# A streaming-encoder layer on one core: u projected first by neighbouring tokens and turned through DRAM, v second

## The chip, the core and the metric

The kernel runs on one core of a Trainium2 chip. The metric is the device time of one execution in microseconds (us), the median of several runs; less is better. A core has a matrix engine (TensorE, PE in the profile; its weight loads are listed apart as PEld), a vector engine (VectorE, DVE), an activation engine (ScalarE, ACT), a general engine (GpSimd, POOL) and a queue engine (SyncE, SP) that only issues transfers. Each engine works its instructions off in the order in which the program lists them. ScalarE and GpSimd can issue transfers too; such an instruction then stands in that engine's own order.

## What is computed

One residual layer of 1024 tokens with 1024 channels: two parallel token mixers on one normalised input, then cross-attention into 256 memory tokens, then a gated MLP. What matters here is the first projection and what is done with two of its parts.

```python
h = rms_norm(x, norm_mix_pre)                  # x * rate(token) * gain(channel)
q, k, v, u, gate_logits = split(h @ w_in)      # v and u: 512 columns each
o_attn = stick_breaking_attention(q, k, v)
ug = u.reshape(1, S, 32, 16)                   # 32 groups of 16 channels
bu = einsum('gpc,bsgc->bsgp', b_bar, ug)       # then a scan over the 1024 tokens
o_ssm = ...                                    # read out, + d * u, gelu, GLU
```

The rate of a token (one over the root of its mean square) is a factor of a whole row of h, so the kernel multiplies with it after the product, not before.

## The kernel before, in words

Every float32 product is made of three matmuls of rounded halves: `mm3` (L141) multiplies high by high (L142), high by low (L143) and low by high (L144). The first stage holds the transposed input `hT` (channels on the partitions, tokens along the row) and makes two passes over it. In a pass, `tokens(now, n, i, k)` (L427) is called for 8 token tiles i and 8 channel tiles k. 128 columns of `hT` are the stationary operand, 512 columns of weights the moving one, and the sum lies in one of six PSUM banks `ps_m`. So one pass has 8 x 8 x 3 = 192 matmuls of 128x512.

- Pass n = 0 makes v. Tile i takes tokens i*128 to i*128+127, which lie side by side in `hT`. `put` (L438) has ScalarE scale the sum by the rates of the tile (`rates_x`, one per partition) into a row buffer `vr` (L443), and SP writes it to DRAM (`v_d`, L444). Attention loads it from there much later (`values`, L985).
- Pass n = 1 makes u. The state-space branch wants eight neighbouring tokens in one partition. So tile i takes the tokens i, i+8, i+16, ... (`slice(i, S, 8)`, L429), whose columns of `hT` lie 8 elements (32 bytes) apart, and `put` writes straight into the tile `U` (L440). Its rates are needed in the same order: they go from `rates_x` to DRAM (`rx_d`, L409) and come back as `r8` (L410).

`rates_out` (L406) also issues the load of `row_k` (L411, issued at L280), a row of rates that attention needs later. `mem_rates_out` (L505) writes the rates of the memory tokens to DRAM. All these are issued by SP.

The four weight chunks of each pass come through four buffers (tag `wr`, `w_load` L378). ScalarE rounds them to the high half (L389) and VectorE makes the low half (L393). The two tiles of the memory tokens (`mem_load`, L495) use the same four buffers afterwards.

While the second pass runs on PE, VectorE and ScalarE prepare the state-space tables (`tables` L644, `operators` L663, `readout` L675). After it PE runs gate projections (`gate_job` L284, weights cast at L256, low half at L260), and between them in fixed slots the state-space steps: `flip_u` (L715) transposes groups of `U`, `states` (L730) multiplies and starts a scan on VectorE (L744 to L756), `outputs` (L762) reads it out.

The order of the work on PE, ScalarE, VectorE and GpSimd is written out by hand: `at(t, go)` (L228) puts a piece of work on a list with a planned time, and `all_events` (L232) emits the list in the order of these times. The planned times fix the order only; an engine starts its next instruction as soon as what it waits for is there. The order on SP is chosen by the compiler's own scheduler.

The times that the change uses are planned times too. The second pass begins at `u_begin` (52.4), the chunks' low halves are planned from L819 on, and the pass ends about 47 later.

Of the kernel before, what the change touches and what calls it, by code (L numbers as in the profile page):

```python
# [11 lines left out]
F32 = mybir.dt.float32  # L12
F32R = mybir.dt.float32r
BF16 = mybir.dt.bfloat16
AF = mybir.ActivationFunctionType
# [5 lines left out]
P = 128  # L21
S = 1024
# [23 lines left out]
def kernel(ctx: ExitStack, tc: tile.TileContext, a: dict, out: bass.AP, dbg=None):  # L46
    nc = tc.nc
    V, G, C, T = nc.vector, nc.gpsimd, nc.scalar, nc.tensor
    dma = nc.sync.dma_start
# [3 lines left out]
    dpool = ctx.enter_context(tc.tile_pool(name="dpool", bufs=1, space=DRAM))  # L53
    ha = ctx.enter_context(tc.tile_pool(name="ha", bufs=4, side="left"))

    v_d = dpool.tile([S, 512], F32, name="v_d")
    os_d = dpool.tile([4, P, S], F32, name="os_d")
    oa_d = dpool.tile([4, P, S], F32, name="oa_d")
    ol_d = dpool.tile([4, P, S], F32, name="ol_d")
# [9 lines left out]
    zcol = const.tile([P, 1], F32, name="zcol")  # L69
# [7 lines left out]
    wr = ExitStack()  # L77
    pr_ = wr.enter_context(tc.tile_pool(name="pr", bufs=1, side="left"))
    row_k = pr_.tile([P, 512], F32, name="row_k")
    gcol = pr_.tile([P, 2, KT], F32, name="gcol")  # L80
    rates_x = pr_.tile([P, 2, KT], F32, name="rates_x")
    rates_m = pr_.tile([P, 2], F32, name="rates_m")
    pr_.tile([P, 88], F32, name="pad_r")
    rx_d = dpool.tile([KT, P], F32, name="rx_d")
    rm_d = dpool.tile([2, P], F32, name="rm_d")
# [16 lines left out]
    def ps(tag):  # L102
        pool, w, n = psum[tag]
        return pool.tile([P, w], F32, tag=tag, name="ps_" + tag, bufs=n)
# [36 lines left out]
    def mm3(acc, sh, sl, mh, ml, first, last):  # L141
        T.matmul(acc, sh, mh, start=first, stop=False)  # L142
        T.matmul(acc, sh, ml, start=False, stop=False)  # L143
        T.matmul(acc, sl, mh, start=False, stop=last)  # L144
# [83 lines left out]
    def at(t, go):  # L228
        heapq.heappush(events, (t, len(seen), go))
        seen.append(t)  # L230
# [48 lines left out]
    def rates_load(h):  # L279
        dma(row_k, rx_d[4 * h:4 * h + 4].rearrange("t p -> (t p)").partition_broadcast(P))  # L280
# [57 lines left out]
    def h_hi(k, sl):  # L338
        return hT[0][k // 4][:, k % 4, sl]

    def h_lo(k, sl):
        return hT[1][k // 4][:, k % 4, sl]

    def g3(ap):
        return ap.rearrange("p (g c) -> p g c", c=16)

    wx = ExitStack()
    px = wx.enter_context(tc.tile_pool(name="px", bufs=1, side="left"))
# [3 lines left out]
    pa = ra.enter_context(tc.tile_pool(name="pa", bufs=1, side="right"))  # L352
    r0 = ExitStack()
    p0 = r0.enter_context(tc.tile_pool(name="p0", bufs=1, side="right", reuse_waits="tile"))
# [4 lines left out]
    U = pa.tile([P, 32, 8, 16], F32, name="U")  # L359
# [4 lines left out]
    xt, rows_x, raw, pair = {}, {}, {}, {}  # L364
# [12 lines left out]

    def w_load(n, c):  # L378
        raw[n, c] = px.tile([P, 1024], F32, tag="wr", name="wr", bufs=4)
        dma(raw[n, c], a["w_in_N"][n, c])  # L380

    def w_pair(n, c):
        if c == 3:
# [17 lines left out]
        V.tensor_scalar(r, sums_x[:, t:t + 1], 1.0 / D, EPS, op0=ALU.mult, op1=ALU.add)  # L401
        G.tensor_tensor(rates_x[:, 0, t:t + 1], r, mhalf, op=ALU.pow)

    r8 = pa.tile([P, 8], F32, name="r8")

    def rates_out():  # L406

        V.tensor_scalar(rates_x[:, 1], rates_x[:, 0], -1.0, None, op0=ALU.mult)
        dma(rx_d.rearrange("t p -> p t"), rates_x[:, 0])  # L409
        dma(r8, rx_d.rearrange("t (q r) -> (t q) r", r=8))  # L410
        rates_load(0)  # L411

    def gained(t, kk):
        ks = slice(0, KT) if kk is None else slice(4 * kk, 4 * kk + 4)
# [11 lines left out]

    def tokens(now, n, i, k):  # L427

        sl = slice(i * P, (i + 1) * P) if n == 0 else slice(i, S, 8)  # L429
        if k == 0:  # L430
            accs_[n, i] = ps("m")
        acc = accs_[n, i]
        wh, wl = (w[:, (k % 2) * 512:(k % 2 + 1) * 512] for w in pair[n, k // 2])
        mm3(acc, h_hi(k, sl), h_lo(k, sl), wh, wl, k == 0, k == KT - 1)
        if k < KT - 1:
            return

        def put(t):  # L438
            if n:
                C.activation(U[:, :, i, :], g3(acc), AF.Identity, bias=zcol, scale=r8[:, i:i + 1])  # L440
                return
            vt = p0.tile([P, 512], F32, tag="vr", name="vr", bufs=3)
            C.activation(vt, acc, AF.Identity, bias=zcol, scale=rates_x[:, 0, i:i + 1])  # L443
            dma(v_d[i * P:(i + 1) * P, :], vt)  # L444

        at(now + STEP + (0.2 if n else 7.0), put)

# [28 lines left out]
    def begin_of(t):  # L476
        return FIRST + 16 * STEP + 8 * STEP * (t - 2)

    u_begin = begin_of(KT)

    for t in range(KT):
        s0 = begin_of(t)
        if t > 1:
            for kk, go, dt_ in ((None, gained, 3.6), (0, x_high, 2.35), (1, x_high, 1.75), (0, x_low, 1.7), (1, x_low, 1.0)):
                at(s0 - dt_, lambda _, go=go, t=t, kk=kk: go(t, kk))
        if t + 4 < KT:
            at(s0 + (2.0 if t > 1 else 12.0), lambda _, t=t: x_load(t + 4))
# [15 lines left out]
        G.tensor_tensor(rates_m[:, i:i + 1], r, mhalf, op=ALU.pow)  # L503

    def mem_rates_out():  # L505
        dma(rm_d.rearrange("t p -> p t"), rates_m)

    line(70.0, (lambda: mem_load(0), 0), (lambda: mem_load(1), 16.0), (lambda: mem_rate(0), 1.4), (lambda: mem_rate(1), 2.6),
         (mem_rates_out, 0))
# [16 lines left out]
    turns = pa.tile([P, 7, 32], F32, name="turns")  # L526
    pr = pa.tile([P, 32, 9], F32, name="pr")
    pi = pa.tile([P, 32, 9], F32, name="pi")
    pa.tile([P, 96], F32, name="pad_a")

    def constants():
        G.memset(ec, math.e)
# [282 lines left out]
    u_begin = clock  # L815
# [58 lines left out]
    while timed:  # L874
        t0, _, took, go, n = heapq.heappop(timed)
# [70 lines left out]
    for m in range(4):  # L946
        j = glu_job(m)
# [165 lines left out]
    t, nf, begun, last_z = 0.0, 0, {}, 1e9  # L1113
# [393 lines left out]
    for n, (ch, go, args, last) in enumerate(steady):  # L1507
        while timed and timed[0][0] <= clock + STEP / 2:
            _, _, took, turn_, x = heapq.heappop(timed)
# [17 lines left out]
    while timed:  # L1527
        _, _, took, turn_, x = heapq.heappop(timed)
# [633 lines left out]
    for s in range(last + 1):  # L2162
        prep()
        w, r = 1 + s // 7, s % 7
# [60 lines left out]
    for prod in (2, 1, 5, 6, 3, 7):  # L2225
        acc = bank_b if prod in (2, 5, 3) else bank_a
        for k in range(NF // 2):
# [11 lines left out]
            elif i2 == 4:  # L2239
# [3 lines left out]
                r8 = ExitStack()  # L2243
# [107 lines left out]
```

## Time and profile before

| | us |
|---|---|
| median of 3 runs | 1651.96 (1651.85 to 1652.86) |
| the profiled execution | 1653.66 |
| its span, first to last instruction | 1651.9 |
| PE busy in it | 1632.3 |
| VectorE busy in it | 1163.5 |
| ScalarE busy in it | 880.3 |
| mean granted TensorE clock | 0.996 of full speed |

The profile comes from one execution. It lists busy time by engine, groups of instructions by line, the waits between engines, and a timeline. In a timeline row stand the start, the length, the engine, the line, the operation, what is written and read, and in brackets how long the engine had been idle and what ended that. Times in the views count from the first instruction.

### The profile page before, as it was taken

Reading aid. Unit: us, or ns where it says so; the run is one execution under the profiler, and the core shown is the slowest. Engines: PE = TensorE matmul, PEld = TensorE weight load, DVE = VectorE, ACT = ScalarE, POOL = GpSimd, SP = SyncE. Lnnn points to the kernel's source line nnn. Section 1 sums busy time; section 2 is a strip of 40 time slices with the busy share of each in tenths; the row PEclk is TensorE's granted clock in tenths of the full one; section 3 lists DMA queues with packets and bytes.
Section 4 is the critical chain, followed back from the end, with each engine's and each line's share of the span. In section 5 each row is a group of like instructions: output and inputs, shape, how many; then the busy total and the mean of one; then the engine's idle time right before and its main releaser. Section 6 shows DMA issues by size and latency. Waiting matters only on the chain.

```text
span 1651.9 us, 22414 instructions
## 1 busy us (share of the span) xinstructions
PE 1632.3 (99%) x8062; PEld 1383.0 (84%) x8062; DVE 1163.5 (70%) x1616; ACT 880.3 (53%) x1459; POOL 202.2 (12%) x296
## 2 busy tenths in 40 slices
PE   9999999999999999999999999999999999999998
PEld 7998888888888988888888888878888888888886
DVE  7778637776867688467555678888887788775473
ACT  5434346676766544345444556556555556654441
POOL 5000002333332000011000000111111111000010
PEclk9999999999999999999999998999999999999999
DMA  9412144232433964464323684677777676688672
GB/s 328 120 46 66 59 145 111 71 102 78 115 99 125 334 198 134 166 217 153 140 65 128 225 274 153 194 207 214 210 198 201 186 203 187 208 301 290 192 236 82
DMA packets 125439, 279.26 MB, mean 169 GB/s; under 512 B 23696, under 2 KB 28304, under 8 KB 125200
## 3 DMA queue, kind: packets, MB, share of 16 engines
q1 hardware_dynamic: 113664, 251.35, 46.2%
q0 software_dynamic: 9360, 18.09, 6.2%
q10 hardware_dynamic: 2304, 8.39, 1.3%
q8 instruction: 63, 1.03, 0.3%
q14 instruction: 48, 0.39, 0.1%
HBM read 203.98 MB, written 67.38 MB: 164 GB/s over the span
## 4 chain that ended last, share of the span: by engine, by line
PE 90%; DVE 5%; DMA 2%; ACT 2%; issue 1%; SPq 0%; POOL 0%; DVEq 0%; ACTq 0%; POOLq 0%
PE ps_p L1928 8%; PE ps_p L1927 8%; PE ps_p L1926 8%; PE ps_f L142 7%; PE ps_f L144 6%; PE ps_f L143 6%; PE ps_d L2198 4%; PE ps_d L2196 4%; PE ps_d L2197 4%; PE ps_m L143 3%; PE ps_m L142 3%; PE ps_m L144 3%; PE ps_o L1070 2%; PE ps_w L1045 2%; PE ps_z L142 1%; PE ps_z L144 1%
## 5 line engine op out<-in xcount | busy, mean ns | idle before, releaser
L142 PE MATMUL ps_f<-hT,wh 128*128 128x512 f32 x384 | 161.2, 420 | 0.0
L144 PE MATMUL ps_f<-hT,wl 128*128 128x512 f32 x384 | 150.8, 393 | 0.0
L143 PE MATMUL ps_f<-hT,wh 128*128 128x512 f32 x384 | 150.6, 392 | 0.0
L1927 PE MATMUL ps_p<-qS,bm 128*128 128x512 f32 (+2 forms) x368 | 141.5, 384 | 1.7 <-DVE qS L1751 1.7
L1926 PE MATMUL ps_p<-qS,bm 128*128 128x512 f32 (+2 forms) x368 | 141.4, 384 | 1.0 <-DVE uu L1944 1.0
L1928 PE MATMUL ps_p<-qS,bm 128*128 128x512 f32 (+2 forms) x368 | 141.5, 384 | 0.0
L148 DVE TENSOR_TENSOR dn<-raw,dn 128x1024 fp32r<-128x1024 f32 x77 | 93.6, 1223 | 63.6 <-ACT dn L147 61.1
L147 ACT CAST dn<-raw 128x1024 fp32r<-128x1024 f32 x77 | 80.6, 1052 | 86.9 <-PE ps_d L2198 40.0
L2196 PE MATMUL ps_d<-dn 128*128 128x512 f32 x308 | 119.8, 389 | 0.0
L2197 PE MATMUL ps_d<-dn 128*128 128x512 f32 x308 | 119.8, 389 | 0.0
L2198 PE MATMUL ps_d<-dn 128*128 128x512 f32 x308 | 119.8, 389 | 0.0
L1031 POOL TENSOR_TENSOR s<-s,s 128x127 f32<-128x127 f32 (+4 forms) x96 | 89.8, 936 | 223.1 <-DVE s L1025 175.5
L1928 PE MATMUL ps_p<-qA,bm 128*128 128x512 f32 (+2 forms) x272 | 105.3, 387 | 0.5 <-DVE bm L1857 0.5
L1926 PE MATMUL ps_p<-qA,bm 128*128 128x512 f32 (+2 forms) x272 | 105.5, 388 | 0.0
L1927 PE MATMUL ps_p<-qA,bm 128*128 128x512 f32 (+2 forms) x272 | 105.3, 387 | 0.0
L1939 ACT COPY uu<-ps_p 128x512 f32<-128x512 f32 (+2 forms) x90 | 51.5, 572 | 92.3 <-PE ps_p L1928 92.3
L1869 POOL DMA_DIRECT2D bm<-in_ffn_up_T x61 | 52.7, 864 | 358.7 <-ACT bm L1868 149.6
L144 PEld LDWEIGHTS ps_f<-hT,wl 128*128 128x128 f32 x384 | 72.1, 188 | 16.1
L1019 ACT ACTIVATE s<-ps_z,rates_x 128x128 f32<-128x128 f32 (+3 forms) x96 | 56.3, 586 | 53.7 <-PE ps_z L1008 48.2
L1927 PEld LDWEIGHTS ps_p<-qS,bm 128*128 128x128 f32 x368 | 70.2, 191 | 15.0 <-DVE qS L1751 2.0
L1926 PEld LDWEIGHTS ps_p<-qS,bm 128*128 128x128 f32 x368 | 70.1, 191 | 14.5 <-ACT uu L1939 1.4
L1928 PEld LDWEIGHTS ps_p<-qS,bm 128*128 128x128 f32 x368 | 70.3, 191 | 13.3 <-DVE bm L1857 0.2
(544 smaller groups left out, 4459.5 us busy)
## 6 DMA issues: line engine op xcount, KB each, us to landing
raw<-sd SPq DMA_DIRECT2D x77, 256.0 KB, 4.0
bm<-in_ffn_up_T POOLq DMA_DIRECT2D x61, 256.0 KB, 5.4
ws<-in_w_in_T SPq DMA_DIRECT2D x24, 512.0 KB, 3.5
ws<-in_xa_wo_N SPq DMA_DIRECT2D x23, 512.0 KB, 4.1
wv<-in_ffn_up_T SPq DMA_DIRECT2D x22, 512.0 KB, 4.1
wg<-in_ffn_up_T SPq DMA_DIRECT2D x22, 512.0 KB, 3.9
dr<-in_ffn_down SPq DMA_DIRECT2D x22, 512.0 KB, 6.6
td<-st SPq DMA_DIRECT2D x44, 256.0 KB, 6.1
```

Of the source, the lines that this page charges most:

```text
L142: T.matmul(acc, sh, mh, start=first, stop=False)
L143: T.matmul(acc, sh, ml, start=False, stop=False)
L144: T.matmul(acc, sl, mh, start=False, stop=last)
L147: C.copy(dh, src)
L148: (lo or V).tensor_tensor(dl, src, f(dh), op=ALU.subtract)
L1031: G.tensor_tensor(s1[:, n0:e], s1[:, n0:e], s2[:, n0 + 1:e + 1], op=ALU.mult)
L1926: T.matmul(acc, bm[:, 0, ks], q[:, 0, k, cs], start=alone and k == 0, stop=False, skip_group_check=True)
L1927: T.matmul(acc, bm[:, 0, ks], q[:, 1, k, cs], start=False, stop=False, skip_group_check=True)
L1928: T.matmul(acc, bm[:, 1, ks], q[:, 0, k, cs], start=False, stop=k == 3, skip_group_check=True)
L2196: T.matmul(acc[i], v[:, 0, 0, sl], v[:, 0, 1], start=first, stop=False, skip_group_check=True)
L2197: T.matmul(acc[i], v[:, 0, 0, sl], v[:, 1, 1], start=False, stop=False, skip_group_check=True)
L2198: T.matmul(acc[i], v[:, 1, 0, sl], v[:, 0, 1], start=False, stop=last, skip_group_check=True)
```

## The change

Pass n = 0 now makes u and pass n = 1 makes v: the weights are taken in the other order, and both passes take neighbouring tokens. The rows of u are written to a new DRAM tensor `u_d` from the first pass. Four loads (`steps_load`, SP) bring them back with eight neighbouring tokens per partition, 128 columns each, through the `wr` buffers, and four copies on ScalarE (`steps_put`) put them into `U`. The rows of v go to `v_d` from the second pass through one buffer `vt`, which the gate projections use after it. `r8` and its load are gone. The write of the token rates, the load of `row_k` and the write of the memory rates are issued by ScalarE, the first two at later planned times. A padding tile grows by what `r8` took.

```diff
     v_d = dpool.tile([S, 512], F32, name="v_d")
+    u_d = dpool.tile([S, 512], F32, name="u_d")
...
     def w_load(n, c):
         raw[n, c] = px.tile([P, 1024], F32, tag="wr", name="wr", bufs=4)
-        dma(raw[n, c], a["w_in_N"][n, c])
+        dma(raw[n, c], a["w_in_N"][1 - n, c])
...
-    r8 = pa.tile([P, 8], F32, name="r8")
-
     def rates_out():
 
         V.tensor_scalar(rates_x[:, 1], rates_x[:, 0], -1.0, None, op0=ALU.mult)
-        dma(rx_d.rearrange("t p -> p t"), rates_x[:, 0])
-        dma(r8, rx_d.rearrange("t (q r) -> (t q) r", r=8))
-        rates_load(0)
+        at(60.0, lambda _: C.dma_start(rx_d.rearrange("t p -> p t"), rates_x[:, 0]))
+        at(78.0, lambda _: C.dma_start(row_k, rx_d[0:4].rearrange("t p -> (t p)").partition_broadcast(P)))
...
-        sl = slice(i * P, (i + 1) * P) if n == 0 else slice(i, S, 8)
+        sl = slice(i * P, (i + 1) * P)
...
         def put(t):
-            if n:
-                C.activation(U[:, :, i, :], g3(acc), AF.Identity, bias=zcol, scale=r8[:, i:i + 1])
-                return
-            vt = p0.tile([P, 512], F32, tag="vr", name="vr", bufs=3)
+            vt = (pa.tile([P, 512], F32, tag="vt", name="vr", bufs=1) if n else
+                  p0.tile([P, 512], F32, tag="vr", name="vr", bufs=3))
             C.activation(vt, acc, AF.Identity, bias=zcol, scale=rates_x[:, 0, i:i + 1])
-            dma(v_d[i * P:(i + 1) * P, :], vt)
+            dma((v_d if n else u_d)[i * P:(i + 1) * P, :], vt)
...
+    rows_u = {}
+
+    def steps_load(o):
+
+        rows_u[o] = px.tile([P, 8, 128], F32, tag="wr", name="ur", bufs=4)
+        dma(rows_u[o], u_d[:, 128 * o:128 * o + 128].rearrange("(j r) c -> j r c", r=8))
+
+    def steps_put(o):
+        C.copy(U[:, 8 * o:8 * o + 8].rearrange("p g r c -> p r g c"), rows_u[o].rearrange("p r (g c) -> p r g c", c=16))
+
+    for o in range(4):
+        at(u_begin + (14.0, 16.5, 27.5, 33.5)[o], lambda _, o=o: steps_load(o))
+        at(u_begin + (24.0, 30.0, 36.0, 42.0)[o], lambda _, o=o: steps_put(o))
...
     def mem_rates_out():
-        dma(rm_d.rearrange("t p -> p t"), rates_m)
+        C.dma_start(rm_d.rearrange("t p -> p t"), rates_m)
...
-    pa.tile([P, 96], F32, name="pad_a")
+    pa.tile([P, 104], F32, name="pad_a")
```

## The prediction

> **What bounds the kernel now.** I read the page first: the span and the busy times.
>
> ```profile
> span 1651.9 us, 22414 instructions
> PE 1632.3 (99%) x8062; PEld 1383.0 (84%) x8062; DVE 1163.5 (70%) x1616; ACT 880.3 (53%) x1459; POOL 202.2 (12%) x296
> ```
>
> PE is busy in all but 20 us of the span. So time can be won only where PE works slower than it could, or where it waits. The view of who waited for whom, for PE alone, has these two rows in the part that is changed:
>
> ```profile
> PE ps_m L770 <- DVE rc L756: 0.7, 1, 0.7
> PE ps_m L143 <- DVE wl L393: 0.6, 1, 0.6
> ```
>
> Neither is removed by the edit: one is the state-space scan on VectorE, the other the low half of the second pass's first chunk. What the edit can win must be pace. So I read the timeline of PE through both passes and the gate projection behind them.
>
> ```profile
> 20.00 0.39 PE L142 MATMUL ps_m<-wx,hT 128*128 128x512 f32 x1
> ...
> 53.14 0.40 PE L144 MATMUL ps_m<-wx,hT 128*128 128x512 f32 x1
> ...
> 54.38 0.64 PE L143 MATMUL ps_m<-wl,hT 128*128 128x512 f32 x1 [0.60 <-DVE wl L393]
> ...
> 60.01 0.41 PE L144 MATMUL ps_m<-wx,hT 128*128 128x512 f32 x1
> ...
> 69.88 0.41 PE L142 MATMUL ps_m<-wh,hT 128*128 128x512 f32 x1
> ...
> 104.64 0.39 PE L142 MATMUL ps_f<-hT,wh 128*128 128x512 f32 x1
> ...
> 112.18 0.39 PE L142 MATMUL ps_f<-hT,wh 128*128 128x512 f32 x1
> ...
> 117.62 0.39 PE L142 MATMUL ps_f<-hT,wh 128*128 128x512 f32 x1
> ```
>
> The starts give the pace. First pass: 146 steps from 20.00 to 53.14, 0.2270 us each. Second pass, with tokens 8 apart: 40 steps from 60.01 to 69.88, 0.2467 each. Gate projection: 24 steps from 112.18 to 117.62, 0.2267 each. All are 128x512 matmuls. The groups of PEld show the difference that goes with it. First between 20 and 48 us:
>
> ```profile
> L143 PEld LDWEIGHTS ps_m<-wl,hT 128*128 128x128 f32 x31 | 5.8, 188 | 1.2
> ```
>
> and then between 53 and 99 us:
>
> ```profile
> L143 PEld LDWEIGHTS ps_m<-wl,hT 128*128 128x128 f32 x43 | 14.2, 331 | 0.9 <-DVE wl L393 0.9
> ```
>
> A load of neighbouring columns takes 188 ns, one of columns 32 bytes apart 331 ns. In the stages view neither the clock nor the transfers explain it (columns: window, its length, PE busy, granted clock, transfer share, GB/s): the slow pass has the full clock and hardly a transfer.
>
> ```profile
> 20.00:53.00 33.00, 33.00 (x147) 1.00 0.86 314
> 55.00:77.00 22.00, 22.00 (x91) 1.00 0.38 85
> 80.00:97.40 17.40, 17.40 (x72) 1.00 0.01 1
> ```
>
> **The change, part by part.** *The second pass takes neighbouring tokens.* 192 matmuls go from 0.2467 to the 0.2267 of the gate projection, the nearest row with quiet transfers: 192 x 0.0200 = 3.84 us. With the first pass's 0.2270 it would be 3.78. I take 3.8. All of it is on PE's own path. The first pass keeps its pace and its loads, only with the other half of the weights.
>
> *The 0.60 us stall at 54.38 stays.* It ends with VectorE's low half, and the edit removes nothing ahead of that on VectorE. Were it to vanish, it would add 0.6; I count nothing.
>
> *Puts.* Eight scaled copies go to a row buffer and eight writes are added (u); v's eight move later. To see what ScalarE has room for, its timeline:
>
> ```profile
> 64.31 0.78 ACT L440 ACTIVATE U<-ps_m,zcol,r 128x512 f32<-128x512 f32 x1 [9.01 <-DMA r<-rx_d]
> ...
> 88.69 0.19 ACT L501 ACTIVATION_READ_ACCUMULATOR wr<-wr 128x1 f32 x1
> ...
> 97.86 0.78 ACT L440 ACTIVATE U<-ps_m,zcol,r 128x512 f32<-128x512 f32 x1 [5.13 <-PE ps_m L144]
> ...
> 100.19 1.05 ACT L256 CAST wh<-ws 128x1024 fp32r<-128x1024 f32 x1
> 104.84 0.78 ACT L440 ACTIVATE U<-ps_m,zcol,r 128x512 f32<-128x512 f32 x1 [3.60 <-PE ps_m L144]
> 105.51 1.04 ACT L256 CAST wh<-ws 128x1024 fp32r<-128x1024 f32 x1
> ```
>
> The 9.01 us for the returned rates go, but PE never waited for them, since six PSUM banks take the sums: nothing. The copies into `U` are 128x1024. The cast of that size takes 1.05. A copy with scattered elements, the nearest dear row, took 1.1 for half of that:
>
> ```profile
> 136.11 2.19 ACT L788 COPY U<-ps_m 128x512 f32<-128x512 f32 x2 [1.43 <-PE ps_m L786]
> ```
>
> So four copies cost 4.2 to 8.8 us. The runs here are 16 elements long, as in the put into `U` at 0.78, so I take the low end. ScalarE waits 3 to 9 us before each put, and only its work after 96 has a deadline on PE: nothing.
>
> *Transfers.* The sizes and times to landing, from the list of transfers:
>
> ```profile
> g_d<-glog SPq DMA_DIRECT2D x32, 256.0 KB, 2.0
> ...
> v_d<-vr SPq DMA_DIRECT2D x8, 256.0 KB, 5.8
> ...
> vv<-v_d SPq DMA_DIRECT2D x8, 256.0 KB, 3.3
> ```
>
> and from the list for 20 to 120 us:
>
> ```profile
> wr<-in_mem SPq DMA_DIRECT2D x2, 512.0 KB, 6.5
> ...
> rx_d<-rates_x SPq DMA_DIRECT2D x1, 4.0 KB, 11.1
> ```
>
> A load of u is 512 KB in 1024 pieces of 512 bytes: between 3.3 (256 KB in as many pieces) and 6.5; I take 5. The last put of u is planned behind v's first, whose sum is ready at 54.4 + 23 x 0.2267 = 59.6. So the last row of u lands at about 66 at the latest, and the first load by 72. Its copy is planned behind v's fourth put, near 54.4 + 95 x 0.2267 = 75.9. The third load needs the first one's buffer, the fourth the second's. The second copy is planned behind v's fifth put (81.4) and three table passes of the cast's size after it, 3.2 us: the buffer is free at about 85, the load there by 90, copied at about 95. Covered.
>
> *The single buffer of v's rows.* This is the added wait that matters: put i+1 stands on ScalarE until write i has landed, and behind it stand the tables' sines, the copies and the casts of the gate weights. A put's circle is 0.78 for the put, 0.4 for SP's issue (0.33 in a row below, and the step between engines), and the landing. A tile of the pass lasts 24 x 0.2267 = 5.44. So the circle fits when a write lands within 4.2 us. The write of the same shape in quiet hours takes 2.0, v's writes among the loads of the first pass 5.8. The stages above show 0.38 and then 0.01 of the transfers' time in use; the change adds 4 MB there. I take 2.0 to 4: nothing.
>
> *Queue moves.* Two of SP's waits go:
>
> ```profile
> SPq L506 <- POOL rates_m L503: 24.7, 1, 24.7
> ...
> SPq L410 <- DMA rx_d<-rates_x: 10.1, 1, 10.1
> ```
>
> SP stood there with v's writes and later the gate weights behind it, which PE did not miss. On ScalarE each issue costs about 0.33:
>
> ```profile
> L1427 ACTq DMA_DIRECT2D x_d<-y x8: 326/326/344, 716.9 to 783.9; - x8
> ```
>
> The load of `row_k` waits for the rates to be in DRAM: issued near 61, landed by 72 at 11.1, and ScalarE gets to it after 76. The write of the memory rates could hold ScalarE until GpSimd has them:
>
> ```profile
> 89.25 1.58 POOL L503 TENSOR_TENSOR rates_m<-mr,mhalf 128x1 f32<-128x1 f32 x2 [15.00 <-DVE mr L502]
> ```
>
> GpSimd is done at 90.8, the squares on ScalarE (above) at 88.9. So it stands 1.9 us at most, and the third copy of u lies between. Behind it wait v's seventh put at about 94.5 and the cast at about 97, both later than 90.8: nothing.
>
> *Does the gain survive the seam?* The first gate projection needs a cast and a low half. VectorE's rows:
>
> ```profile
> 94.32 0.69 DVE L673 TENSOR_TENSOR W<-W,tq 128x512 f32<-128x512 f32 x1
> 101.27 1.23 DVE L260 TENSOR_TENSOR wl<-ws,wh 128x1024 fp32r<-128x1024 f32 x1 [6.25 <-ACT wh L256]
> 106.58 1.23 DVE L260 TENSOR_TENSOR wl<-ws,wh 128x1024 fp32r<-128x1024 f32 x1 [4.09 <-ACT wh L256]
> ```
>
> VectorE idles 6.25 us there, more than the shift of 3.8, and both casts follow PE. Low half done at 102.5, needed at 104.64: 2.1 us to spare now. From 106.58 on VectorE is nearly always busy; it waits for PE once, and PE's own 0.7 wait for the scan later shows that this chain sets the pace for a while:
>
> ```profile
> 123.68 0.69 DVE L744 TENSOR_TENSOR bp<-ps_m,cosT 128x512 f32<-128x512 f32 x1 [0.68 <-PE ps_m L735]
> ```
>
> But its head waits for the second cast, behind the last put, which waits for PE: the chain moves with PE.
>
> Sum: -3.8. The profiled execution took 1653.66, 1.76 more than its span, and lies 1.70 above the median. Its own time would become 1649.9, the median 1651.96 - 3.8 = 1648.2, or 0.23% less. About 0.2%, 3.3 us, is what a measurement can tell from no change here: the forecast lies just past it.
>
> **The rivals.** *One, the gain is handed back at the seam (about the same time).* SP's order is the scheduler's. If the fourth load of u is listed behind the write of v's seventh tile, SP issues it only after that put, at 97.86 - 3.3 + 0.8 = 95.3 (3.3 is 167 of the matmuls at 0.02). It lands at 100.3, its copy ends at 101.4, the cast, planned behind the copy, at 102.4, the low half at 103.7, and PE, ready at 100.8, waits 2.9. Time 1648.2 + 2.9 = 1651.1. For it: SP stood 24.7 us at one instruction before. Against: the buffer is free by about 84, ten us earlier.
>
> *Two, the single buffer sets the pace (slower).* If v's writes land in L us, the circle is L + 1.2, and from L = 4.2 on every put falls back: at the eighth, by 7 x (L - 4.2). With 5.8 that is 11.2 us. The casts stand behind the puts, so the scan chain and then PE are late by it, less the 0.7 us of VectorE's wait for PE in the chain: 1648.2 + 11.2 - 0.7 = 1658.7. It is slower than before from L = 4.9 on (7 x 0.7 = 4.9), by over 0.2% from 5.3. For it: the 5.8 of the same write. Against: that was among 314 GB/s, and 2.0 stands for the same shape later.
>
> *Three, no gain.* The slow pace has a cause that stays, such as ScalarE and VectorE reading beside it. Then 1652.0. Against: the gate projection at 112 has VectorE as busy and runs at 0.2267.
>
> The Trainium skill, page "TensorE: Matmul & The Clock Gate", section "Part 2: What happens when you issue a matmul", gives a reason for the third: loads of the next weights run beside the current matmul through a read port of their own and cost it nothing. By that rule the load's 331 ns would be hidden and the result would be 1652.0; the trace disagrees, 0.2467 against 0.2267.
>
> **How the numbers follow.** Forecast 0.60, rival one 0.24, two 0.11, three 0.05. The likeliest is 1648.2. Its low end: both stalls of PE gone as well, 1648.2 - 0.6 - 0.7 = 1646.9. The high end takes in rival one with a load that lands at 5.4 instead of 5: 1651.5. Two and most of three stay outside, about 0.15. Faster by over 0.2% means below 1648.66: nine tenths of the forecast case, 0.55. Within 0.2%: the rest of it, one and three, 0.34. Slower: 0.11.
>
> **What would show it.** Right: PEld at about 188 ns in both passes, a pace of 0.227 in the second, the first gate matmul at 100.8 instead of 104.64, the 0.60 stall still there, and the shift of 3.8 unchanged at the end of the state-space part. Wrong: a wait of PE for the first gate low half (rival one); ScalarE waiting for writes of `v_d` ahead of its puts, or the wait for the scan growing (two); 0.2467 as before (three).

## The result and the profile after

The changed kernel takes 1656.95 us, median of 11 runs (1653.43 to 1660.33). The kernel before took 1652.12 beside it (11 runs, 1650.38 to 1653.27). The ratio is 1.0028, 95% interval 1.002 to 1.0035: the change makes the kernel slower by 4.8 us.

The profiled execution of the changed kernel is the fastest of its 11, 1653.43. First its page and the view of who waited for whom, PE alone (line, releaser line; us in total, times, longest). Line numbers are those of the kernel that ran: in the changed kernel up to 10 away from those of the kernel before, in the experiments up to 37.

```profile
span 1651.6 us, 22444 instructions
PE 1627.8 (99%) x8062; PEld 1368.8 (83%) x8062; DVE 1162.7 (70%) x1616; ACT 883.6 (53%) x1463; POOL 202.0 (12%) x296
```

```profile
PE ps_m L745 <- ACT Ug L732: 2.3, 1, 2.3
PE ps_m L780 <- DVE rc L766: 1.5, 2, 0.9
PE ps_f L143 <- ACT wh L257: 0.5, 1, 0.5
PE ps_f L145 <- DVE wl L261: 0.5, 1, 0.5
```

PE is busy 4.5 us less than before, as a faster second pass would have it, but the span is the same: PE waits instead. The two rows of 0.5 are the first gate projection, the row of 2.3 the first state multiplication (`states`), and the wait for the scan (L780) has grown from 0.7 to 1.5. All four lie behind the second pass.

**The pass itself is as fast as hoped.** A group of PEld between 5 and 99 us (both passes together), then PE's timeline:

```profile
L144 PEld LDWEIGHTS ps_m<-wl,hT 128*128 128x128 f32 x96 | 18.0, 188 | 4.9 <-DVE wl L394 0.7 <-DVE wl L459 0.5
```

```profile
53.47 0.50 PE L144 MATMUL ps_m<-wl,hT 128*128 128x512 f32 x1 [0.24 <-DVE wl L394]
...
59.28 0.39 PE L145 MATMUL ps_m<-wh,hT 128*128 128x512 f32 x1
...
70.38 0.39 PE L143 MATMUL ps_m<-wh,hT 128*128 128x512 f32 x1
...
100.39 0.50 PE L143 MATMUL ps_f<-hT,wh 128*128 128x512 f32 x1 [0.55 <-ACT wh L257]
101.64 0.50 PE L145 MATMUL ps_f<-hT,wl 128*128 128x512 f32 x1 [0.52 <-DVE wl L261]
...
107.04 0.39 PE L145 MATMUL ps_f<-hT,wl 128*128 128x512 f32 x1
109.74 1.29 PE L745 MATMUL ps_m<-Ug,E 128*128 128x128 f32 x8 [2.31 <-ACT Ug L732]
...
111.26 0.63 PE L144 MATMUL ps_f<-hT,wh 128*128 128x512 f32 x1
...
113.82 0.50 PE L144 MATMUL ps_f<-hT,wh 128*128 128x512 f32 x1
...
257.28 0.22 PE L1017 MATMUL ps_z<-k,q 128*128 128x128 f32 x1
```

A load takes 188 ns in both passes, and 49 steps from 59.28 to 70.38 are 0.2265 each. The first gate matmul starts at 100.39, where it was 104.64: 4.2 us won, and 0.55 of waiting lies in it already. Then it goes wrong: three waits, and after the one of 2.31 us a stretch in which each matmul lasts 0.63 instead of 0.39. Six steps from 111.26 to 113.82 take 0.427 each; at 0.227 they would have taken 1.2 us less. The stages view (window, length, PE busy, granted clock, transfer share, GB/s) has the clock for it:

```profile
105.00:110.00 5.00, 2.69 (x13) 1.00 0.43 145
110.00:115.00 5.00, 5.00 (x20) 0.66 0.24 55
115.00:120.00 5.00, 5.00 (x24) 1.00 0.64 166
```

So a stand of 2.3 us is paid for a second time, by half again, at the lower clock behind it. The Trainium skill, page "TensorE: Matmul & The Clock Gate", section "Part 1: The HAM clock gate (the "warmup" mystery)", says that the array falls to half rate after an idle window of about 3.4 us and needs about as long a busy one to come back. The trace agrees on the halving and roughly on the way back (0.427 from about 110.7 to 113.8), but a stand of 2.31 was enough.

The last row is the first score of attention (`ps_z`), the end of the part that is changed. It stood at 255.47 before; a second profiled execution of the same changed kernel, told below, has it at 261.26. I use this start as the measure of the seam, because the rest, to the first matmul of the last projection, took 1177.6 to 1181.4 us in the 13 profiled executions here, in no order by kernel. In the profiled execution above the later part happened to be 2.5 us shorter than in that of before (1177.6 against 1180.07), which is why its span looks unharmed.

**Where the seam is lost.** ScalarE's timeline around the second pass, `ACTq` being transfers that it issues:

```profile
59.03 0.78 ACT L439 ACTIVATE vr<-ps_m,zcol,rates_x 128x512 f32<-128x512 f32 x1 [4.25 <-PE ps_m L145]
59.13 0.39 ACTq L408 DMA_DIRECT2D rx_d<-rates_x  x1
...
71.27 0.78 ACT L439 ACTIVATE vr<-ps_m,zcol,rates_x 128x512 f32<-128x512 f32 x1 [10.79 <-DMA v_d<-vr]
...
78.25 0.78 ACT L439 ACTIVATE vr<-ps_m,zcol,rates_x 128x512 f32<-128x512 f32 x1 [5.26 <-DMA v_d<-vr]
78.93 1.05 ACT L670 ACTIVATE sinT<-x 128x1024 f32<-128x1024 f32 x1
...
96.20 0.38 ACTq L516 DMA_DIRECT2D rm_d<-rates_m  x1
96.70 0.78 ACT L439 ACTIVATE vr<-ps_m,zcol,rates_x 128x512 f32<-128x512 f32 x1 [3.58 <-POOL rates_m L513]
...
107.49 0.78 ACT L439 ACTIVATE vr<-ps_m,zcol,rates_x 128x512 f32<-128x512 f32 x1 [7.16 <-PE ps_f L145]
```

The second put of v waits 10.79 us for the buffer `vr`, that is, for the first write to `v_d`. In the chain of waits that write and v's second are one row each, and the list of transfers from 54 to 104 us has the two rate writes (KB each, median us from issue to landing):

```profile
59.83 11.33 DMA v_d<-vr
...
72.89 5.25 DMA v_d<-vr
```

```profile
rx_d<-rates_x ACTq DMA_DIRECT2D x1, 4.0 KB, 11.2
...
rm_d<-rates_m ACTq DMA_DIRECT2D x1, 1.0 KB, 9.4
```

The token rates' write, 1024 pieces of 4 bytes, is issued at 59.13 and takes 11.2, to 70.3; the write of v issued 0.7 us behind it lands at 71.16. The last row of u, written at 60.50, is held in the same way (10.8 us), and SP stands for it before it can issue the first two loads of u (SP's waits):

```profile
SPq L482 <- DMA u_d<-vr: 10.5, 1, 10.5
```

So these loads, 512 KB each, leave at 71.46 instead of 62.44 as in the kernel `rows` below, just ahead of v's second write, which then takes 5.25 us (4.0 in `rows`). That is the 5.26 of the third put: the second half of the delay on ScalarE comes from bytes, but the first hold put them there. At the other end the memory rates' write is issued at 96.20, v's seventh write 1.3 us later; that one lands after 9.9, and the last put waits until 107.49. (Its row blames PE, which had ended that sum long before: the profile puts a wait for two things down to the later by its records. In the second execution the same row blames the write, as shown there.)

What hangs on these two waits shows on VectorE:

```profile
80.23 2.38 DVE L665 TENSOR_TENSOR x<-x,turns 128x8 f32<-128x8 f32 x7 [12.34 <-POOL x L662]
...
99.66 0.69 DVE L683 TENSOR_TENSOR W<-W,tq 128x512 f32<-128x512 f32 x1
100.36 1.22 DVE L261 TENSOR_TENSOR wl<-ws,wh 128x1024 fp32r<-128x1024 f32 x1
```

The sines of the tables stand behind the third put on ScalarE, so they come at 78.93, and GpSimd and VectorE, which build the tables from them, are late. VectorE ends the tables at 100.35; before, the row at 94.32 was its last. The first low half follows at once, done at 101.6, 1.2 us after PE had begun that projection.

### The profile page after: what moved, and what is told of

It is laid out like the page before. It is cut to its first block, busy times and chain, and to the rows that moved or that the text cites. A ratio compares the mean times of both kernels' runs of the same rounds, so it can differ in the third digit from the quotient of the medians.

```text
span 1651.6 us, 22444 instructions
## 1 busy us (share of the span) xinstructions
PE 1627.8 (99%) x8062; PEld 1368.8 (83%) x8062; DVE 1162.7 (70%) x1616; ACT 883.6 (53%) x1463; POOL 202.0 (12%) x296
## 3 DMA queue, kind: packets, MB, share of 16 engines
q8 instruction: 63, 1.03, 0.3%
## 4 chain that ended last, share of the span: by engine, by line
PE 84%; DVE 8%; DMA 4%; ACT 2%; issue 2%; SPq 0%; POOL 0%; DVEq 0%; ACTq 0%; POOLq 0%
PE ps_p L1936 7%; PE ps_p L1937 7%; PE ps_p L1938 7%; PE ps_f L143 6%; PE ps_f L145 6%; PE ps_f L144 6%; PE ps_d L2208 4%; PE ps_d L2206 4%; PE ps_d L2207 4%; PE ps_m L144 2%; PE ps_m L145 2%; PE ps_m L143 2%; PE ps_o L1080 2%; PE ps_w L1055 2%; PE ps_z L143 1%
```

## The experiments

Two theories stood against each other at first. The landing theory: the scattered 4-byte writes hold the writes of v, and the single buffer passes that on to everything behind it on ScalarE. Its rivals: the pace gain is not worth what was thought; or the new order itself (u's copies and the rates' issues on ScalarE) makes the seam late, whatever the landings. A score start below is that of `ps_z` in the one profiled execution, and what it gains or loses is against 255.47.

| kernel | median (range), us | before beside it | ratio (95%) | first gate matmul | first score |
|---|---|---|---|---|---|
| after | 1656.95 (1653.43 to 1660.33) | 1652.12 | 1.0028 (1.002 to 1.0035) | 100.39 | 257.28 |
| pace | 1648.58 (1645.72 to 1650.56) | 1652.45 | 0.9977 (0.9967 to 0.9987) | 99.7 | 250.47 |
| rows | 1649.32 (1647.47 to 1651.24) | 1652.45 | 0.9981 (0.9972 to 0.9989) | 99.77 | 250.58 |
| two | 1648.32 (1647.72 to 1649.52) | 1652.45 | 0.9973 (0.9963 to 0.9983) | 100.07 | 250.86 |
| early | 1650.18 (1647.0 to 1658.0) | 1652.45 | 0.999 (0.998 to 1.0001) | 100.09 | 251.75 |
| sp | 1658.79 (1658.02 to 1662.12) | 1652.77 | 1.0043 (1.0029 to 1.0056) | 108.24 | 261.36 |
| early_rm | 1657.78 (1656.12 to 1659.8) | 1652.77 | 1.0033 (1.002 to 1.0046) | 99.42 | 259.87 |
| both | 1650.61 (1648.84 to 1652.06) | 1652.77 | 0.9985 (0.9977 to 0.9994) | 99.75 | 250.53 |
| rx_only | 1656.94 (1655.03 to 1658.19) | 1651.8 | 1.0028 (1.0016 to 1.0039) | 107.49 | 258.3 |
| rx_alone | 1654.98 (1650.89 to 1657.84) | 1652.49 | 1.0012 (1.0002 to 1.0022) | 100.22 | 255.68 |

Two more ran once each: `again` (1659.65) and `land` (1650.3).

### pace: the kernel before, with neighbouring tokens in both passes

```diff
-        sl = slice(i * P, (i + 1) * P) if n == 0 else slice(i, S, 8)
+        sl = slice(i * P, (i + 1) * P)
```

> The kernel before with one edit: the second pass takes neighbouring tokens too (u then holds the wrong tokens; nothing else moves). Theory A (the pace gain is real and is lost to the transfers): 3.8 us less than before, about 1648.2, with weight loads of 188 ns in the second pass. Theory C (the pace is no gain, or the seam takes it back by itself): 1651.5 or more.

Measured: 3.9 us faster than before, score start 5.0 earlier. The loads between 5 and 99 us:

```profile
L143 PEld LDWEIGHTS ps_m<-wl,hT 128*128 128x128 f32 x96 | 18.0, 188 | 4.6 <-DVE wl L463 0.5 <-DVE wl L393 0.3
```

The pace gain is real and arrives at the end. So the rest of the change costs 1656.95 - 1652.12 + 3.9 = 8.7 us.

### rows: the same two rate transfers, but as rows of 512 bytes

Both rates are turned on PE, copied by ScalarE and written as 8 and 2 rows; queue and single buffer stay. The places shift a little: the token rates are issued at 60.58, now behind v's first write (59.63), the memory rates at 91.19.

```diff
-        at(60.0, lambda _: C.dma_start(rx_d.rearrange("t p -> p t"), rates_x[:, 0]))
+        def turned(_):
+            tp = ps("m")
+            T.transpose(tp[:KT, :P], rates_x[:, 0], ident)
+            at(60.0, lambda _: sent(tp))
+        def sent(tp):
+            C.copy(row_k[:KT, :P], tp[:KT, :P])
+            C.dma_start(rx_d, row_k[:KT, :P])
+        at(59.0, turned)
...
-        C.dma_start(rm_d.rearrange("t p -> p t"), rates_m)
+        tp = ps("m")
+        T.transpose(tp[:2, :P], rates_m, ident)
+        def sent(_):
+            C.copy(raw["m", 0][:2, :P], tp[:2, :P])
+            C.dma_start(rm_d, raw["m", 0][:2, :P])
+        at(91.0, sent)
```

> The changed kernel, but the token rates and the memory rates are turned by a transpose on PE and leave as rows of 512 bytes in place of 1024 and 256 pieces of 4 bytes; queue, place and the single buffer stay. Theory A (a write of 4-byte pieces in flight holds up the landing of v's rows, and the single buffer hands that to ScalarE): the first and the seventh write of v land in 2 to 4 us, ScalarE's waits for v's rows are gone, 1648 to 1649. Theory B (v's rows land late because of the loads of u in 512-byte pieces and of the memory tokens, whatever the rates do): waits of 5 us and more stay, 1653 or more. Theory C: above 1651.

Measured: 1649.32, 3.1 us faster than before and just above the range of theory A. ScalarE's puts on either side:

```profile
64.41 0.78 ACT L448 ACTIVATE vr<-ps_m,zcol,rates_x 128x512 f32<-128x512 f32 x1 [3.86 <-PE ps_m L145]
...
69.90 0.78 ACT L448 ACTIVATE vr<-ps_m,zcol,rates_x 128x512 f32<-128x512 f32 x1 [3.76 <-PE ps_m L145]
...
100.02 0.78 ACT L448 ACTIVATE vr<-ps_m,zcol,rates_x 128x512 f32<-128x512 f32 x1 [2.77 <-PE ps_m L145]
```

The second put waits for PE at 64.41, not for a write until 71.27, the third likewise, and the last one starts 7.5 us sooner. PE's waits at the seam are gone but for the old 0.7 for the scan. Since the token rates are issued here 0.95 us behind v's first write, that write alone would be no test. But the first loads of u (62.44) and v's second write (65.22) leave within 5 us of the rates and land in 4.9 and 4.0 us, where scattered rates held u's last row for 10.8. With the queue, the single buffer and nearly the same order, the form of the two writes decides; the rival of the order falls.

### two: the scattered writes stay, v's rows get a second buffer

```diff
-            vt = (pa.tile([P, 512], F32, tag="vt", name="vr", bufs=1) if n else
+            vt = row_k if n and i % 2 else (pa.tile([P, 512], F32, tag="vt", name="vr", bufs=1) if n else
...
-        at(78.0, lambda _: C.dma_start(row_k, rx_d[0:4].rearrange("t p -> (t p)").partition_broadcast(P)))
+        at(120.0, lambda _: C.dma_start(row_k, rx_d[0:4].rearrange("t p -> (t p)").partition_broadcast(P)))
```

The second buffer is the tile `row_k`, so the load of `row_k` moves to 120.

> The changed kernel, but v's rows take turns in two buffers (the second is the still unused row of rates, loaded later instead); all transfers stay. Theory A: the first write still takes 11 us to land, but ScalarE waits for it 1 us at most, and the last put waits for nothing: 1648 to 1649.5. Theory B: the writes between the loads of u are slow too; two buffers hide up to 9 us each, so it helps as much. If the lateness comes from SP's order or from ScalarE's own copies, it stays above 1653.

Measured: 1648.32, the lowest median of all, 4.1 us below before; the score starts 4.6 earlier. The waits of ScalarE for v's writes, 50 to 130 us:

```profile
ACT vr L439 <- DMA v_d<-vr: 5.6, 2, 5.0
ACT row_k L439 <- DMA v_d<-row_k: 1.8, 1, 1.8
```

The slowest write of v still takes 11.2 us to land, but only the third put needs that buffer, and it stands 5.0 us where the second stood 10.8. So both halves are needed for the loss: a late landing and a single buffer.

### early: the token rates leave at once on SP, as before the change

```diff
-        at(60.0, lambda _: C.dma_start(rx_d.rearrange("t p -> p t"), rates_x[:, 0]))
+        dma(rx_d.rearrange("t p -> p t"), rates_x[:, 0])
```

> The changed kernel, but the write of the token rates is issued by SP as soon as they are known, as before, some 8 us earlier; the memory rates stay on ScalarE. Theory A: the first wait of 10.8 us shrinks to 0 to 3 and VectorE is in time again, but the memory rates' write still holds up the seventh write of v at the seam: the last put is late by about 4, so about 1651 to 1653. Theory B: no change against the changed kernel, 1655 to 1658.

Measured: 1650.18, a little under the range of theory A and 2.3 us below before by the medians; but the interval includes 1, so a gain is not shown, and one run of the 11 reached 1658.0. The write is issued at 50.75, well ahead of v's first, and holds a row of u instead (11.3 us). Of the first puts only the third waits for a write, 5.07 us for v's second, which lands in 5.8 beside the loads of u. The hold at the memory rates stays:

```profile
96.32 0.78 ACT L439 ACTIVATE vr<-ps_m,zcol,rates_x 128x512 f32<-128x512 f32 x1 [6.07 <-DMA v_d<-vr]
```

The write it waits for was issued at 89.34, 0.34 us ahead of the memory rates, and took 6.9: a write just in front can be held too. (In `two` the write in that place, 0.23 ahead, landed in 2.1.) Moving the large scattered write away from v's first writes takes away most of the loss, 251.75 against 257.28 at the score.

### sp: all three transfers back on SP, the rest of the change kept

```diff
-        at(60.0, lambda _: C.dma_start(rx_d.rearrange("t p -> p t"), rates_x[:, 0]))
-        at(78.0, lambda _: C.dma_start(row_k, rx_d[0:4].rearrange("t p -> (t p)").partition_broadcast(P)))
+        dma(rx_d.rearrange("t p -> p t"), rates_x[:, 0])
+        at(78.0, lambda _: dma(row_k, rx_d[0:4].rearrange("t p -> (t p)").partition_broadcast(P)))
...
-        C.dma_start(rm_d.rearrange("t p -> p t"), rates_m)
+        dma(rm_d.rearrange("t p -> p t"), rates_m)
```

> The changed kernel with its queue part undone: all three rate transfers are SP's again, in the places that the scheduler gives them (the token rates early, the memory rates ahead of the sixth write of v). Theory A (the 4-byte pieces in flight hold up v's rows, whichever queue issues them): like the kernel with the early write, 1649 to 1653, with waits of ScalarE for v's rows near 66 to 72 and at the seam. If the queue itself were the cause, the waits would be gone: 1648 to 1649.

Measured: 6.0 us slower than before, far above the 1649 to 1653 of theory A, though its waits are there (6.48 and 6.40 us at the second and third put, and the seam). PE's longest wait at the seam, and ScalarE's put that makes it:

```profile
PE ps_f L143 <- ACT wh L257: 8.4, 1, 8.4
```

```profile
104.56 0.78 ACT L439 ACTIVATE vr<-ps_m,zcol,rates_x 128x512 f32<-128x512 f32 x1 [14.68 <-DMA v_d<-vr]
```

On SP the memory rates' write waits 6.2 us for GpSimd with v's write behind it (issued at 93.04 and 93.51), v's write then takes 10.9 to land, and the single buffer passes both on: 14.68 us at one put. Earlier SP stands 10.5 us at the load of `row_k` until the token rates have landed, with the last rows of u and v's first behind it. So the holds come with either queue, and the queue itself is not the cause. Whether the move to ScalarE's queue gained anything is not shown: the median is 1.2 us worse than that of the changed kernel against before, but the two intervals overlap, and the score starts at 261.36 here and at 261.26 in the second execution of the changed kernel.

### early_rm: early, and the memory rates written behind the last put

```diff
-         (mem_rates_out, 0))
+    at(112.0, lambda _: mem_rates_out())
```

> The kernel with the early write of the token rates, but the memory rates are written only behind the last put of v. Theory A: the wait at the seam is gone too, the first one of about 5 stays but is covered: 1648 to 1649, and the spread of the runs shrinks to about 3. If something else makes the seam late (the fourth load or copy of u): 1650 or more, as with the early write alone.

Measured: 5.0 us slower than before, where I had expected a gain: a miss. No put of v waits for that write now, but the next thing does.

```profile
105.68 0.38 ACTq L516 DMA_DIRECT2D rm_d<-rates_m  x1
...
119.63 0.58 ACT L290 COPY glog<-ps_f 128x512 f32<-128x512 f32 x1 [13.44 <-DMA g_d<-glog]
```

The gate logits go out through the same single buffer (`vt`), one write each, and the write of the first, issued 1.8 us behind the rates, is held like v's: it lands after 12.0 us, some 4 past the rates themselves (9.7). The second logits' copy stands 13.44 us, the copy `Ug` behind it is late, and PE waits 5.0 for that. I had moved the write, not the cause.

### rx_only and rx_alone: only the token rates scattered

In both the token rates' write stays as in the change, and the memory rates go as rows. In `rx_only` PE turns them where `rows` does, in `rx_alone` behind the last put; the diff is that of `rx_alone`.

```diff
-        C.dma_start(rm_d.rearrange("t p -> p t"), rates_m)
+        at(102.0, turned_m)
+    def turned_m(_):
+        tp = ps("m")
+        T.transpose(tp[:2, :P], rates_m, ident)
+        def sent(_):
+            C.copy(stage_m[:2, :P], tp[:2, :P])
+            C.dma_start(rm_d, stage_m[:2, :P])
+        at(103.5, sent)
```

> The changed kernel with the memory rates turned on PE and sent as rows; the token rates still leave in 1024 pieces of 4 bytes at the changed place. It parts the loss between the two writes. Theory A: the first wait of 10.8 us on v's row buffer stays, VectorE's tables are 5 to 6 us late and PE waits about 1 for the first gate job's low half, but the last put waits for nothing: first score of attention at 251.5 to 253.5 (250.6 with both as rows, 257 to 261 in the changed kernel), 1649 to 1651.5. If the memory rates do no harm of their own: as the changed kernel, 1656 and above.

> The write of the token rates alone, mended: the memory rates are turned on PE only behind the last put of v, where PE waits for nothing, and leave as rows. The token rates leave in 4-byte pieces at the changed place. Theory A: first wait of 10 to 11 us on v's row buffer, VectorE's tables 5 to 6 us late, a PE wait of about 1 at the first gate job, no wait of the last put; first score of attention at 251.5 to 253.5, 1649 to 1651.5. If the first write alone makes the whole loss: 256 and above, 1655 or more.

`rx_only` came out 5.1 us slower than before, but by my edit: VectorE's delay makes the memory rates late, and PE's transpose of them stood 6.2 us in PE's own order (`ps_m` waiting for GpSimd's `rates_m`), and half clock followed (0.63 us long from 97.30 on), so the first gate matmul came at 107.49. It does not part the two writes. `rx_alone` mends that and misses theory A's ranges: it lies between the two expectations, close under the second one, 2.5 us slower than before, its 11 runs spread from 1650.89 to 1657.84. PE's timeline:

```profile
102.65 0.50 PE L145 MATMUL ps_f<-hT,wl 128*128 128x512 f32 x1 [1.82 <-DVE wl L261]
...
103.84 0.63 PE L143 MATMUL ps_f<-hT,wh 128*128 128x512 f32 x1
...
105.98 0.63 PE L145 MATMUL ps_f<-hT,wl 128*128 128x512 f32 x1
```

The first hold alone (11.0 us here) makes VectorE late for the first low half. PE stands 1.82 us and then works at half clock, five steps of 0.428 from 103.84 to 105.98. No hold follows at the last put, and PE has no further wait but the old 0.7 for the scan: score start 255.68, where 250.6 to 250.9 stand without holds. Set beside `early`, which has mainly the other hold (2.3 us faster than before), and `rows` with neither (3.1 faster), the medians put the token rates' write at 2.5 + 3.1 = 5.6 us and the memory rates' write at 0.8; the two together are 4.8 + 3.1 = 7.9. This is an estimate: by the table each of these medians is known to about 1.5 us either way, so the 5.6 is clear of noise and the 0.8 is not.

### both: rows and two together

Edits as above.

> Rates as rows of 512 bytes and two buffers for v's rows: both cures together. Theory A: nothing is left to win over either one, 1648 to 1649, and the transpose on PE costs about 0.3. Theory B: a gain over each, to 1647 or less.

Measured: 1650.61, above the 1648 to 1649 expected and 2.2 us below before; score start 250.53, that of `rows`. The second remedy adds nothing to the first; the medians of `rows`, `two` and `both` differ by up to 2.3 us, with overlapping intervals.

### again: the changed kernel a second time

> The changed kernel once more, for a second profile. Its median is 3.5 us above its profiled execution. Theory A: the same three waits (first write of v, memory rates, last put), and the spread comes from how long PE stands at the seam and runs at half clock behind it: with a longer span, more matmuls of over 0.6 us near 110. If the spread comes from elsewhere, the seam looks the same and the time sits in a later stage.

Measured: 1659.65. The first projection waits 1.04 and 0.53 instead of 0.55 and 0.52, and half clock sets in at once (103.86, 0.63 long) and a second time at 124.52, behind a wait of the scan chain:

```profile
PE ps_m L780 <- POOL x L662: 2.2, 1, 2.2
PE ps_m L745 <- ACT Ug L732: 1.5, 1, 1.5
PE ps_f L143 <- ACT wh L257: 1.0, 1, 1.0
```

ScalarE's last put, where the row of the first execution blamed PE:

```profile
110.08 0.78 ACT L439 ACTIVATE vr<-ps_m,zcol,rates_x 128x512 f32<-128x512 f32 x1 [7.88 <-DMA v_d<-vr]
```

The same holds cost 4 us more at the score. Which wait crosses into half clock differs between executions, which goes some way to explain the spread of the changed kernel (6.9 us).

### land: what about the writes is slow

The kernel `rows`, in which nothing holds, and five more writes that nothing reads, on ScalarE's queue beside the gate projections: the memory rates scattered as in the change, the token rates scattered as in the change, the same 1024 pieces 64 bytes apart, the same 512 bytes apart, and the same bytes as 128 pieces of 32 bytes side by side.

```diff
+    at(124.0, lambda _: C.dma_start(dn1.rearrange("t p -> p t"), rates_m))
+    at(140.0, lambda _: C.dma_start(dn4.rearrange("t p -> p t"), rates_x[:, 0]))
+    at(160.0, lambda _: C.dma_start(sp16[:, :, 0:1].rearrange("t p o -> p t o"), rates_x[:, 0].unsqueeze(2)))
+    at(175.0, lambda _: C.dma_start(sp128[:, :, 0:1].rearrange("t p o -> p t o"), rates_x[:, 0].unsqueeze(2)))
+    at(190.0, lambda _: C.dma_start(dn8.rearrange("t p -> (t p)").rearrange("(p t) -> p t", t=KT), rates_x[:, 0]))
```

> The kernel with rates as rows, plus five writes that nobody reads, on ScalarE's queue between about 110 and 200 us: 256 pieces of 4 bytes side by side, 1024 of them side by side, 1024 at a pitch of 64 bytes, 1024 at a pitch of 512 bytes, and 128 pieces of 32 bytes. If the number of pieces sets the landing: about 3, 11, 11, 11 and 2 us. If it is pieces that meet in the same stretch of memory: 9, 11, 3, 3 and 2 to 5. The time is that of the added writes and tells nothing else.

The issues and the longer of the two waits that they caused, in ScalarE's timeline:

```profile
122.84 0.39 ACTq L491 DMA_DIRECT2D dn<-rates_m  x1
139.75 0.37 ACTq L492 DMA_DIRECT2D dn<-rates_x  x1
...
152.84 0.59 ACT L290 COPY glog<-ps_f 128x512 f32<-128x512 f32 x1 [9.01 <-DMA g_d<-glog]
...
157.03 0.40 ACTq L493 DMA_DIRECT2D sp<-rates_x  x1
...
174.71 0.37 ACTq L494 DMA_DIRECT2D sp<-rates_x  x1
```

Behind the first (256 pieces of 4 bytes, side by side) the next write of gate logits landed after 11.5 us (ScalarE waited 1.44 for it at 135.06) and the next load of weights, on SP's queue, after 8.8. Behind the second (1024 pieces) a load of weights took 10.1 and the logits held ScalarE for 9.01. The third, again 1024 pieces of 4 bytes but 64 bytes apart, took 3.2 itself, and two writes issued within 2.5 us of it took 2.1 and 2.5. Of the fourth, 512 bytes apart, no landing is recorded; the transfers from 3.8 us behind it on took 1.8 to 2.8. The fifth, issued at 189.16, took 2.2. Thus it is neither the count nor the size of the pieces alone: 4-byte pieces that fall side by side are slow, and they hold reads as well as writes, on the other queue too. Of the two dense ones this trace has no landing of their own, as nothing waits for them. All this is one execution, but the dense writes of the other runs agree with it.

The Trainium skill, page "DMA: Bandwidth & Descriptors", section "Queues, rings and completion order", gives a reason for the hold: a transfer's completion signal lands only after every earlier write of the same DMA engine, across its queues. The runs agree: 11.33 for a write of v on SP's queue behind the rates on ScalarE's, 2.0 for its median in `rows`. It does not by itself cover the write just in front of the rates in `early` (6.9), nor why landings come up to 4 us past that of the rates. That this rule is the cause, and why pieces side by side are slow at all, no run here shows.

## Why the prediction was wrong, point by point

- **Pace: right.** 3.8 was forecast from 192 steps of 0.0200; the pass runs at 0.2265 and 188 ns per load, and the kernel `pace` keeps 3.9 (1652.45 - 1648.58). The rival that the cause might stay is refuted.
- **The stall of 0.60 at the first low half** was to stay; it is 0.24 here, which helps by 0.4, but 0.7 in `two`: it varies between executions.
- **The copies into `U`** were taken at the low end, 4.2 for four; they took 1.03 to 1.05 each.
- **Transfers of u: right in size, wrong in time.** Their loads landed in 4.4 (median; 5 assumed). But "the last row of u lands at about 66 at the latest" failed for the same reason as the step below: it landed at 71.3, the first loads were issued at 71.46, and they met v's second write. Rival one, the fourth load behind v's seventh write, did not occur (that load was issued at 89.45).
- **The step that failed: "I take 2.0 to 4: nothing" for the landing of v's writes in "The single buffer of v's rows".** The window's bytes were quiet around v's first and seventh write, as argued, but these two landings, 11.33 and 9.9 us, were not made by bytes. Its row stood in the prediction, `rx_d<-rates_x`, 11.1 us for 4 KB, and "landed by 72 at 11.1" was used for the load of `row_k`. It was never asked who else is in the air at that time: the first write of v, issued 0.7 us later, behind which the single buffer holds ScalarE. `land` and `rows` show that the neighbours pay; `two` shows that the single buffer passes it on to ScalarE. The trace of the kernel before had the hold too. There SP issued the token rates at 51.28 and a write of v at 51.76; from its list of transfers for 50 to 62 us:

```profile
v_d<-vr SPq DMA_DIRECT2D x1, 256.0 KB, 11.9
```

  With three buffers no put waited for it, and so it was invisible among the waits. The 5.8 that the prediction took for "v's writes among the loads" is a median over eight writes that hides this one.

- **"Queue moves ... nothing" failed with it.** Three issues of 0.33 were priced as time of ScalarE; the price was where they landed. The stand for GpSimd's memory rates was put at 1.9 at most and was 3.58, since the tables were late by then; what hurt more was the hold behind it, until 107.49.
- **Rival two had the right mechanism, with the wrong shape.** Its formula let all seven circles be late by the same amount, for the load of bytes. In fact two writes landed after 11.33 and 9.9 us, a third after 5.25 beside the late loads, and the puts between caught up (waits for a write of 10.79, 5.26 and 0.91, then none until the last). It gave 1658.7; that the median, 1656.95, is near it is luck.
- **The seam.** "VectorE idles 6.25 us there, more than the shift of 3.8" was true of the kernel before and gone in this one: the idle time moved ahead of the tables (12.34 at the turns), and the spare 2.1 us of the first low half became a wait.
- **Not foreseen at all:** that short stands of PE are followed by a stretch at half clock, some 1.5 us in the first execution.

Account of the seam in the profiled execution, from the first gate matmul to the first score: 150.83 before (255.47 - 104.64), 156.89 after. Of the 6.06 more, the waits for the low half, for `Ug` and for the scan are 0.52, 2.31 and 0.8, half clock 1.2 in the six steps counted and about 0.3 at its edges. The other 0.9 is about what three more stands cost beyond their listed lengths, by an estimate: over the stand of 0.52 the two steps from 100.72 to 101.98 take 1.26, where two take 0.45, so it cost 0.81, or 0.29 more than listed, and three times that is 0.87. In `rows` and `two` the same stretch is 150.81 and 150.79.

The forecast time is reached by `two`, the change with a second buffer for v's rows: 1648.32 against 1652.45 before (0.9973, 0.9963 to 0.9983). Its interval overlaps those of `rows` and `both`, so which of the three is best is not shown.

## What to carry to other kernels

When a small transfer is moved, look not at its bytes but at its landing time, and at every transfer that is issued in the time until it lands: in these runs whatever waited on one of those waited until then or longer. A single buffer between an engine and DRAM turns one late landing into a stand of the whole engine, so give it a second buffer, or write rates and other columns as rows, before giving such a write a place in front of it. And a stand of PE of about 2 us cost more than its length here, because the clock halved behind it.

## What the runs showed of the hardware

- Pieces of 4 bytes side by side in DRAM: 1024 land in 11.1 to 11.5 us, 256 in 8.2 to 10.1; at 64 bytes apart 1024 land in 3.2, and the same bytes as 32-byte pieces in 2.2 (`land`).
- Large transfers issued soon after such a write, loads and writes, land no earlier than it does and up to some 4 us later, whether SP or ScalarE issued the small one: 8.8 to 12.0 us (before, `after`, `early_rm`, `land`) where none held for long in `rows`: 2.0 to 5.4.
- Weight loads of TensorE with columns 32 bytes apart take 331 ns instead of 188 and cost the matmul stream 0.0200 us each, although they are listed as overlapping it (before against `pace`).
- Half clock for about 3 us followed stands of PE of 1.82 us (`rx_alone`), 2.31 (`after`) and 2.18 (`again`), and in `again` two of 1.04 and 0.53 within 1.8 us; behind a stand of 1.47 there the granted clock stayed at 1.00.
